# A tile and a queue of their own for the raw rows of the seven-product units in an FFN down projection

## The chip, the cores and the metric

The kernel runs on one core of one Trainium2 chip. The metric is the device time of one execution in microseconds (us), as the median of several runs. The engines are named as the profile names them: PE is TensorE's matmul side and PEld its weight loads, DVE is VectorE, ACT is ScalarE, POOL is GpSimd, SP is SyncE, which issues most of the DMA loads.

## What is computed

One layer of a decoder trunk over 256 tokens of width 2048, all in float32: a norm, a combined projection, two attentions, gated merging and an output product, then a convolutional gated FFN. The change lies in the FFN's last product. Cut to what matters:

```
def conv_ffn(h, w_up, conv_w, conv_b, w_down):
    a, b = jnp.split(h @ w_up, 2, axis=-1)
    c = conv_b + sum(conv_w[j] * shifted(a, j) for j in range(3))
    return (gelu(c) * b) @ w_down          # (256, 5632) @ (5632, 2048)

x = x + rms_norm(conv_ffn(rms_norm(x, norm_ffn_pre), ...), norm_ffn_post)
```

## The kernel before, in words

**Precision.** Every float32 operand is split into a high part in the fp32r format and a low part, the rest. ScalarE makes the high part (`convert`, L143, "whi"), VectorE subtracts it from the raw values (L144, "wlo"). A product of two split operands is three matmuls: high by high (L175), high by low (L176) and low by high (L177), in `mm3`.

**Order.** The kernel is written with a tile framework. The text of the program gives an order, and the framework's scheduler then orders the instructions of each engine from priorities and modelled times; every engine runs its own list strictly in that order and waits on semaphores. Tiles come from pools: a tile with a tag and `bufs` slots may be written only when the earlier tile in its slot has had all its reads. A helper `at(t, f)` puts off small pieces of work to a later `tick()`; each plain weight row of the stage and each half of a unit of seven ends with one tick.

**Weights.** A raw weight tile holds 128 rows by 1024 columns (512 KB). `raw_row` (L147 to L152) takes one from a ring of three slots (`RAW`) and lets SP load it (L151). Its high and low parts come from rings of four slots (`RING`) with two more under a shared tag; which of raw and converted tiles has these two is set by `flex`, and in the FFN it is the converted ones.

**The FFN.** The up product runs in eleven column blocks of 512 (`ffn_up`), the down product in two parts. After block 5, 24 of the 44 row blocks of w_down are used by `down_pair`, for two pairs of 512 columns each (p = 0 and p = 1); after block 10 the other 20 row blocks follow, and the final norm, whose scale is `gpost2`.

**`down_pair`.** The 24 row blocks are taken in twelve units of two rows. For one unit the product is a 2 x 2 product of blocks: two token halves by two row blocks, and two row blocks by two column halves.
- A *plain* unit (from L1110) converts its two rows and makes 8 products, 24 matmuls, into four accumulators c.
- A unit of *seven* products makes 21 matmuls, by a scheme of the Strassen kind. From its raw rows `even` and `odd` VectorE forms the four differences ta and tb (L1124 to L1127; L1127 writes tb's second half from `odd` and tb's first half). Converted are `odd` whole, the first half of `even`, ta and tb. The products are, in this order: c11 and c12 with odd; q1 with even; q5 and q7 with ta; q6 and c21 with tb. The token sums s1 to s4 that stand on the other side were made earlier (`token_sums`), for the row units 0 to 3; they lie in tiles that take the place of the residual x2.
- After the last unit of seven of a pair, the four q accumulators are combined into the output tiles (L1141 to L1145, "ds"). At the end of the pair the four c accumulators are added (L1155).
- In pair 0 the c accumulators are in the four PSUM banks of the pool `pacc` and the q accumulators in the four others; in pair 1 they are exchanged. The up product's first accumulators ("ua") take `pacc`, its second ("ub") the four others, and are evicted by L1062 and L1063.

The order of the units was the same for both pairs, `PAIR_ORDER = "psppsppsppsp"`, p for plain and s for seven: four units of seven in each pair.

**Around it.** The residual x2 is stored to memory during block 2 by GpSimd (`park`, L1007) and loaded again by SP after the pairs (`unpark`, L1013), as soon as the token sums have been used. GpSimd also loads the scale `gpost2` (L1077) right after block 0, into the tile with the tag "gp", which the scale of the attention's output norm had before. ta and tb share their slots (tags "fa" and "fb") with the evicted up accumulators.

Of the kernel before, what the change touches and what calls it, by code (L numbers as in the profile page):

```python
# [19 lines left out]
P = 128  # L20
D = 2048
# [20 lines left out]
def trunk_layer(ctx, tc, x, x_cols_in, conv_cols_in, g_mix_post, g_ffn_post, w_in, w_q, w_kv,  # L42
                sinks, rel, wo_a, wo_b, w_out, w_up, w_down, rope_tab, strip_sel, out):
    nc = tc.nc
    vec, act, pe, pool = nc.vector, nc.scalar, nc.tensor, nc.gpsimd

    def open_pool(name, bufs=1, **kw):
        es = ExitStack()
        return es, es.enter_context(tc.tile_pool(name=name, bufs=bufs, **kw))
# [9 lines left out]
    def sb(pl, shape, name, dt=F32, tag=None, bufs=None):  # L59
        return pl.tile(shape, dt, name=name, tag=tag or name, **({"bufs": bufs} if bufs else {}))  # L60
# [46 lines left out]
    def ring_tile(kind, name, dt, extra):  # L107
        pl_tag = dict(name=name, tag="flex", bufs=2) if extra else dict(name=name, tag=kind, bufs=RAW if kind == "raw" else RING)
        return ring.tile([P, 1024], dt, **pl_tag)

    def in_turn(kind):

        turn[kind] += 1
        return flex[0] == kind and turn[kind] % (RAW + 2 if kind == "raw" else RING + 1) >= (RAW if kind == "raw" else RING)
# [32 lines left out]
    def raw_row(src):  # L147
        i = cnt[0]
        cnt[0] += 1
        raw = ring_tile("raw", f"raw{i}", F32, in_turn("raw"))  # L150
        nc.sync.dma_start(raw, src)  # L151
        return raw  # L152
# [7 lines left out]
    def tick():  # L160
        for f in steps.pop(now[0], ()):
            f()
        now[0] += 1
# [15 lines left out]
    def gemm(xh, xl, w, k0, nk, c0, n, split=None, extra=None, ps=None):  # L179

        kc = 1024 // n if n in (256, 512) else 2
        acc = new_acc("g", ps)
        todo = []
        cuts = list(range(0, nk, kc)) + [nk]
        for ci, (k, ke) in enumerate(zip(cuts[:-1], cuts[1:])):
            kk = ke - k
            src = w[(k0 + k) * P:(k0 + k + kk) * P, c0:c0 + n].rearrange("(a p) n -> p a n", p=P)
            hi, lo = wchunk(src, [kk, n], *(extra or {}).get(ci, ()))
            for j in range(kk):
                kt = k + j  # L190
                wh, wl = hi[:, j * n:(j + 1) * n], lo[:, j * n:(j + 1) * n]
                for t in range(NT):
                    x_ = [x(k0 + kt)[:, t * P:(t + 1) * P] for x in (xh, xl)]
                    if split is None or t == 0 or ci < split:
                        mm3(acc[t][:, :n], *x_, wh, wl, kt == 0, kt == (split * kc if split and t else nk) - 1)
                    else:
                        todo.append((kt, x_, wh, wl))
            tick()
        return acc, todo
# [377 lines left out]
    acc, _ = gemm(XH, XL, w_in, 0, KT, 0, 512)  # L577
# [4 lines left out]
    acc, _ = gemm(XH, XL, w_in, 0, KT, C_KV, KVR + ROPE)  # L582
# [201 lines left out]
    for j in range(4):  # L784
        acc, _ = gemm(XH, XL, w_in, 0, KT, C_GA + 512 * j, 512)
# [15 lines left out]
    es6, p6 = open_pool("p6")  # L801
# [33 lines left out]
    for j in range(4):  # L835
        ld = merge_loads(j)
        acc, _ = gemm(AH, AL, wo_a, 0, KT, 512 * j, 512)
# [124 lines left out]
    def ffn_up0():  # L962

        sa = [[None, None], [None, None]]

        def evac(acc, q):
            f = sb(p6, [P, 1024], f"f{q}_0", tag="f" + "ab"[q], bufs=2)
            for t in range(NT):
                a = f[:, t * 512:(t + 1) * 512]
                act.activation(a, acc[t], AF.Copy, scale=rf[t][q][:, 0:1])  # L970
                sa[t][q] = a

        def cols(i):
            pt = pst.tile([P, 512], F32, name=f"fT{i}", tag="t")
            for q in range(2):
                for t in range(NT):
                    pe.transpose(pt[:, q * 256 + t * P:q * 256 + (t + 1) * P], sa[t][q][:, i * P:(i + 1) * P], ident)
            conv_cols(i, pt[:, 0:256], pt[:, 256:512], i)

        acc, todo = gemm(HH, HL, w_up, 0, KT, 0, 512, split=0, extra=first_extra)  # L980
        finish_tile(acc[1], todo)
        x2_norm(0)
        x2_norm(1)
        evac(acc, 0)
        drain()
        es8.close()
        esx.close()
        es7, p7 = open_pool("p7")
        g = [slot("b", i) if i < 8 else sb(p7, [P, 1024], f"ghl{i}", F32R) for i in range(12)]
        gT[0][:], gT[1][:] = highs(g), lows(g)  # L990
        dsum_all[:] = [sb(p7, [P, D], f"ds{t}") for t in range(NT)]
        dsum[:] = [[d[:, j * 512:(j + 1) * 512] for j in range(4)] for d in dsum_all]
        norm_row()
        for p in range(8):
            at(now[0] + 1 + (3 * p) // 2, lambda p=p: normed(p, p7))
        acc, _ = gemm(HH, HL, w_up, 0, KT, DFF, 512, ps=(pss, "s"))
        evac(acc, 1)
        for i, w in enumerate((1, 2, 4, 6)):
            at(now[0] + w, lambda i=i: cols(i))
        gtiles[:] = g  # L1000
        s_pool.append(p7)
        return es7
# [70 lines left out]
            at(now[0] + 1 + 2 * i, lambda i=i: conv_cols(4 * c + i, sa[0][i], sa[1][i], slot0 + i))  # L1073

    es7 = ffn_up0()
    gpost2 = sb(p6, [P, D], "gpost2", tag="gp")
    pool.dma_start(gpost2, g_ffn_post.partition_broadcast(P))  # L1077
    for c in range(1, 6):
        if c == 2:
            for i in range(8):  # L1080
# [15 lines left out]
    def down_pair(p):  # L1096

        c11, c12, c21, c22 = c = banks(p, f"c{p}_")
        q1, q5, q7, q6 = q = banks(1 - p, f"q{p}_")
        j0, used = 2 * p, set()  # L1100
        d = [dsum[t][j0 + j] for t in range(NT) for j in range(2)]
        act_of = lambda k, t: (GH(k)[:, t * P:(t + 1) * P], GL(k)[:, t * P:(t + 1) * P])
        row = lambda k: w_down[k * P:(k + 1) * P, j0 * 512:(j0 + 2) * 512]
        half = lambda w, i: tuple(x[:, i * 512:(i + 1) * 512] for x in w)

        def mul(o, x, w, last=False):
            mm3(o, *x, *w, id(o) not in used, last)
            used.add(id(o))

        def plain(u, last):  # L1110
            for k in (2 * u, 2 * u + 1):
                w = convert(raw_row(row(k)), 1024)
                for t in range(NT):
                    for j in range(2):
                        mul(c[2 * t + j], act_of(k, t), half(w, j), last and k % 2 == 1)
                tick()

        def seven(u, last):
            s1, s2, s3, s4 = s_of[u]
            even, odd = raw_row(row(2 * u)), raw_row(row(2 * u + 1))  # L1120
            ta, tb = (sb(p6, [P, 1024], f"t{n}{p}_{u}", tag="f" + n, bufs=2) for n in "ab")
            lo_, hi_ = slice(0, 512), slice(512, 1024)
            w = convert(odd, 1024)
            vec.tensor_tensor(ta[:, lo_], even[:, hi_], even[:, lo_], op=ALU.subtract)  # L1124
            vec.tensor_tensor(ta[:, hi_], odd[:, hi_], even[:, hi_], op=ALU.subtract)
            vec.tensor_tensor(tb[:, lo_], odd[:, hi_], ta[:, lo_], op=ALU.subtract)
            vec.tensor_tensor(tb[:, hi_], odd[:, lo_], tb[:, lo_], op=ALU.subtract)  # L1127
            mul(c11, act_of(2 * u + 1, 0), half(w, 0))
            mul(c12, s4, half(w, 1))
            w = convert(even, 512)  # L1130
            mul(q1, act_of(2 * u, 0), half(w, 0), last)
            w = convert(ta, 1024)
            mul(q5, s1, half(w, 0), last)
            mul(q7, s3, half(w, 1), last)
            tick()
            w = convert(tb, 1024)
            mul(q6, s2, half(w, 0), last)
            mul(c21, act_of(2 * u + 1, 1), half(w, 1))
            tick()
            if last:  # L1140
                act.copy(d[0], q1)  # L1141
                vec.tensor_tensor(d[1], d[0], q6, op=ALU.add)
                vec.tensor_tensor(d[2], d[1], q7, op=ALU.add)
                vec.tensor_tensor(d[3], d[2], q5, op=ALU.add)
                vec.tensor_tensor(d[1], d[1], q5, op=ALU.add)  # L1145

        plain_of, seven_of = iter(range(4, 12)), iter(range(4))
        for i, kind in enumerate(PAIR_ORDER):
            if kind == "s":
                u = next(seven_of)  # L1150
                seven(u, u == 3)
            else:
                plain(next(plain_of), i == len(PAIR_ORDER) - 1)
        for o, x in zip(d, c):
            vec.tensor_tensor(o, o, x, op=ALU.add)  # L1155

    for p in range(2):
        down_pair(p)
    for i in range(8):
        at(now[0] + 40 + 2 * i, lambda i=i: unpark(i // 4, i % 4))  # L1160
    for c in range(6, 11):
# [65 lines left out]


RING = 4
PAIR_ORDER = "psppsppsppsp"  # L1230
XCUT = [0, 1, 2, 3, 4, 6, 8, 10, 12, 14, 16]
X_LOAD = [0, 1, 2, 3, 4, 6, 7, 8, 10]
X_SQ = [4, 4, 5, 5, 6, 7, 8, 9, 10, 11]
# [71 lines left out]
```

## Time and profile before

| What | us |
|---|---|
| median of 3 runs | 1475.07 (1475.04 to 1475.78) |
| the profiled execution's own time | 1475.35 |
| its span in the profile | 1473.5 |
| stage of the two pairs, first product of c to first product of the next ua | 1003.91 to 1132.44 |
| start of the second pair | 1066.49 |

The span is what the profile shows of the program; the 1.85 us between it and the execution's own time lie before and after it. Times within the span are counted from its start. The clock that TensorE was granted is 1.00 in the stage.

How its lines are read: a group or timeline row has the line, the engine, the operation, the tile written, an arrow, the tiles read, the shape, and xN for the number of instructions merged. In the timeline the first number is the start and the second the duration; square brackets hold how long the engine had been idle and what ended that. A matmul's duration is a modelled one of some 0.39 us with the next one overlapping it, so the pace of TensorE is read from the distance of two starts. A row of the waits says who waited for whom, how long in total, how many times, and the longest. SPq is SP's queue of DMA issues; in a row of DMA issues the last number is the median time from issue to landing.

### The profile page before, as it was taken

What the parts mean: (1) busy time and instruction counts of PE and PEld (TensorE: products, weight loads), DVE (VectorE), ACT (ScalarE), POOL (GpSimd) and SP (SyncE); (2) the same over time, 40 slices, a digit from 0 to 9 for tenths busy, and PEclk for the clock granted to TensorE, in tenths of its full rate; (3) what the DMA queues carried; (4) which work ended last, traced back from release to release, by engine and by line L of the source; (5) the groups of instructions that cost most, each with busy time, mean ns of one, the idle gap of its engine ahead of it and who ended that gap; (6) DMA issues with size and microseconds to landing.
All of it is one profiled execution on the core that took longest, in us unless ns stands there. A gap on an engine that the chain in (4) does not pass through costs nothing.

```text
span 1473.5 us, 20861 instructions
## 1 busy us (share of the span) xinstructions
PE 1460.6 (99%) x7591; PEld 1246.1 (85%) x7591; DVE 1026.6 (70%) x1799; ACT 818.3 (56%) x1354; POOL 51.1 (3%) x87
## 2 busy tenths in 40 slices
PE   9999999999999999999999999999999999999997
PEld 7888888888888888888888888888877888888886
DVE  7788874445667665555799877677777676677556
ACT  7588864444565554444666565555444565565443
POOL 0021100000000010000000000000000000000000
PEclk9999999999999999999999999999999999999999
DMA  8755376666655559755766666665667666666653
GB/s 291 223 171 165 94 219 195 206 209 200 186 160 156 171 163 339 224 197 195 224 202 184 192 193 185 188 196 162 209 199 226 210 200 190 194 186 187 198 189 126
DMA packets 154513, 287.58 MB, mean 195 GB/s; under 512 B 18427, under 2 KB 29596, under 8 KB 154284
## 3 DMA queue, kind: packets, MB, share of 16 engines
q1 hardware_dynamic: 149664, 270.43, 59.4%
q0 software_dynamic: 4656, 15.78, 3.4%
q8 instruction: 59, 0.97, 0.3%
q14 instruction: 42, 0.34, 0.1%
q10 hardware_dynamic: 92, 0.05, 0.0%
HBM read 277.79 MB, written 8.44 MB: 194 GB/s over the span
## 4 chain that ended last, share of the span: by engine, by line
PE 92%; DVE 3%; DMA 3%; ACT 1%; issue 0%; DVEq 0%; ACTq 0%; SPq 0%
PE accg L175 15%; PE accg L177 15%; PE accg L176 15%; PE ub L1041 10%; PE ua L1041 10%; PE ua L1045 5%; PE ub L1045 5%; DMA raw<-in_ffn_w_down_dram 2%; PE c L175 1%; PE c L176 1%; PE c L177 1%; DVE wlo L144 1%; PE mpo L760 1%; PE ms L726 1%; PE pt L442 1%; PE qn L691 1%
## 5 line engine op out<-in xcount | busy, mean ns | idle before, releaser
L144 DVE TENSOR_TENSOR wlo<-raw,whi 128x1024 fp32r<-128x1024 f32 (+2 forms) x502 | 604.7, 1207 | 345.4 <-ACT whi L143 340.6
L143 ACT CAST whi<-raw 128x1024 fp32r<-128x1024 f32 (+2 forms) x502 | 518.6, 1036 | 495.7 <-PE accg L177 239.2
L175 PE MATMUL accg<-whi,ahl 128*128 128x512 f32 (+1 forms) x544 | 212.9, 391 | 0.0
L177 PE MATMUL accg<-whi,ahl 128*128 128x512 f32 (+1 forms) x544 | 210.5, 387 | 0.0
L176 PE MATMUL accg<-wlo,ahl 128*128 128x512 f32 (+1 forms) x544 | 209.7, 385 | 0.0
L175 PE MATMUL accg<-whi,bhl 128*128 128x512 f32 x442 | 173.0, 391 | 0.0
L177 PE MATMUL accg<-whi,bhl 128*128 128x512 f32 x442 | 172.3, 390 | 0.0
L176 PE MATMUL accg<-wlo,bhl 128*128 128x512 f32 x442 | 172.2, 390 | 0.0
L1041 PE MATMUL ua<-ahl,whi 128*128 128x512 f32 x640 | 154.8, 391 | 0.9 <-DVE ds L1145 0.9
L1041 PE MATMUL ub<-ahl,whi 128*128 128x512 f32 x640 | 154.6, 391 | 0.0
L1041 PEld LDWEIGHTS ua<-ahl,whi 128*128 128x128 f32 x640 | 117.4, 188 | 24.0 <-DVE ds L1145 1.3
L1041 PEld LDWEIGHTS ub<-ahl,whi 128*128 128x128 f32 x640 | 117.5, 188 | 22.9 <-ACT cc L930 0.3
L177 PEld LDWEIGHTS accg<-whi,ahl 128*128 128x128 f32 x544 | 102.1, 188 | 20.6
L176 PEld LDWEIGHTS accg<-wlo,ahl 128*128 128x128 f32 x544 | 102.3, 188 | 18.1
L175 PEld LDWEIGHTS accg<-whi,ahl 128*128 128x128 f32 x544 | 102.3, 188 | 17.9
L177 PEld LDWEIGHTS accg<-whi,bhl 128*128 128x128 f32 x442 | 83.0, 188 | 17.4
L175 PEld LDWEIGHTS accg<-whi,bhl 128*128 128x128 f32 x442 | 83.0, 188 | 16.9
L176 PEld LDWEIGHTS accg<-wlo,bhl 128*128 128x128 f32 x442 | 83.0, 188 | 16.8
L1045 PEld LDWEIGHTS ub<-ahl,wlo 128*128 128x128 f32 x640 | 82.2, 191 | 3.2
L1045 PEld LDWEIGHTS ua<-ahl,wlo 128*128 128x128 f32 x640 | 82.2, 191 | 3.1
L1045 PE MATMUL ua<-ahl,wlo 128*128 128x256 f32 x640 | 83.7, 283 | 0.0
L1045 PE MATMUL ub<-ahl,wlo 128*128 128x256 f32 x640 | 83.2, 283 | 0.0
(409 smaller groups left out, 1876.1 us busy)
## 6 DMA issues: line engine op xcount, KB each, us to landing
raw<-in_ffn_w_up_dram SPq DMA_DIRECT2D x176, 512.0 KB, 4.5
raw<-in_w_in_dram SPq DMA_DIRECT2D x111, 512.0 KB, 4.4
raw<-in_ffn_w_down_dram SPq DMA_DIRECT2D x88, 512.0 KB, 4.3
raw<-in_w_o_swa_dram SPq DMA_DIRECT2D x32, 512.0 KB, 4.3
raw<-in_w_o_mla_dram SPq DMA_DIRECT2D x32, 512.0 KB, 4.8
raw<-in_w_out_dram SPq DMA_DIRECT2D x32, 512.0 KB, 4.2
bias<-strip POOLq DMA_DIRECT2D x16, 256.0 KB, 4.3
raw<-in_mla_w_q_up_dram SPq DMA_DIRECT2D x32, 128.0 KB, 2.6
```

The lines of the kernel that those rows point to most:

```text
L143: act.copy(hi[:, a:b], raw[:, a:b])
L144: vec.tensor_tensor(lo[:, a:b], raw[:, a:b], hi[:, a:b].bitcast(F32), op=ALU.subtract)
L175: pe.matmul(o, ah, bh, start=start, stop=False)
L176: pe.matmul(o, ah, bl, start=False, stop=False)
L177: pe.matmul(o, al, bh, start=False, stop=stop)
L442: pe.transpose(pt[:, j * P:(j + 1) * P], p[:, c * P:(c + 1) * P], ident)
L691: pe.matmul(o, wl, ch(k), start=False, stop=k == nk - 1)
L726: pe.matmul(o, w, v_, start=n == 0, stop=False)
L760: pe.matmul(o, w(t), p_[:, c], start=n == 0, stop=n == 5)
L1041: pe.matmul(acc[i], hi[:, c], hn[p][:, j * 512:(j + 1) * 512], start=p + j == 0, stop=stop)
L1045: pe.matmul(acc[i][:, 0:256], lo[:, c], hn[p][:, j * 512:j * 512 + 256], start=False, stop=False)
```

## The change

The two raw rows of a unit of seven lie side by side in one tile of 128 x 2048 under the tag "gp" (one slot), and GpSimd loads them as two DMAs of 512 KB. So that the tag is free, the scale's load moves behind both pairs. The order of the units becomes one string for each pair: the first begins with a unit of seven and has four, the second begins with a plain unit as before, has three, and ends on four plain units. The row blocks that are no longer used by a unit of seven go to plain units. All else is the same.

```diff
     es7 = ffn_up0()
-    gpost2 = sb(p6, [P, D], "gpost2", tag="gp")
-    pool.dma_start(gpost2, g_ffn_post.partition_broadcast(P))
     for c in range(1, 6):
...
         def seven(u, last):
             s1, s2, s3, s4 = s_of[u]
-            even, odd = raw_row(row(2 * u)), raw_row(row(2 * u + 1))
+            both = sb(p6, [P, D], f"rr{p}_{u}", tag="gp")
+            even, odd = both[:, 0:1024], both[:, 1024:2048]
+            pool.dma_start(even, row(2 * u))
+            pool.dma_start(odd, row(2 * u + 1))
...
-        plain_of, seven_of = iter(range(4, 12)), iter(range(4))
-        for i, kind in enumerate(PAIR_ORDER):
+        sevens = PAIR_ORDER[p].count("s")
+        plain_of, seven_of = iter(range(sevens, 12)), iter(range(sevens))
+        for i, kind in enumerate(PAIR_ORDER[p]):
             if kind == "s":
                 u = next(seven_of)
-                seven(u, u == 3)
+                seven(u, u == sevens - 1)
             else:
-                plain(next(plain_of), i == len(PAIR_ORDER) - 1)
+                plain(next(plain_of), i == len(PAIR_ORDER[p]) - 1)
...
     for p in range(2):
         down_pair(p)
+    gpost2 = sb(p6, [P, D], "gpost2", tag="gp")
+    pool.dma_start(gpost2, g_ffn_post.partition_broadcast(P))
...
-PAIR_ORDER = "psppsppsppsp"
+PAIR_ORDER = ("sppsppsppspp", "psppsppspppp")
```

In the orders that the scheduler makes, the loads of the first unit's rows stand on GpSimd among the stores of the residual, near where the scale's load stood; the loads of the other six units follow one after another, then the scale's. On SP 14 loads of raw rows are gone and the reloads of the residual stand some places earlier, among the last row loads of pair 1. At the front of pair 0 VectorE has the first unit's odd and even rows and ta ahead of the four evictions of ub, and L1127 and tb's low part behind them; TensorE has one high-part matmul of c21 ahead of q6's low-part one, and three of the next plain row ahead of its first low-part one.

## The prediction

> **What bounds the kernel now.** I read the page first: its span, its busy shares, and the shares of the chain that ended last.
>
> ```profile
> span 1473.5 us, 20861 instructions
> PE 1460.6 (99%) x7591; PEld 1246.1 (85%) x7591; DVE 1026.6 (70%) x1799; ACT 818.3 (56%) x1354; POOL 51.1 (3%) x87
> PE 92%; DVE 3%; DMA 3%; ACT 1%; issue 0%; DVEq 0%; ACTq 0%; SPq 0%
> ```
>
> TensorE carries the end. The change can pay only where TensorE waits inside the stage it touches, the two column pairs of the FFN down product, and it costs at least whatever matmuls it adds. So next I split that stage at the first product of the second pair (windows: time, PE busy, PEld, DVE, ACT, POOL, clock, DMA share, GB/s).
>
> ```profile
> 1003.91:1066.49 62.58, 62.58 (x278) 51.82 (x277) 50.06 (x63) 32.43 (x40) 0.00 (x0) 1.00 0.60 190
> 1066.49:1132.44 65.95, 64.14 (x277) 51.47 (x276) 48.13 (x54) 31.18 (x33) 0.00 (x0) 1.00 0.64 200
> ```
>
> By the code each pair has 8 plain units of 24 matmuls and 4 units of seven products with 21: 276. (The counts include one or two of the neighbours.) The first pair takes 62.58 us, 0.2267 us per matmul. The second, same work and clock 1.00, takes 65.95: **3.37 us of waiting, all in the second pair**. Who is waited for is in TensorE's waits from 1003 to 1136 us, and two of them in the timeline:
>
> ```profile
> PE c L176 <- DVE wlo L144: 1.6, 2, 0.8
> PE ua L1041 <- DVE ds L1145: 0.9, 1, 0.9
> PE q L176 <- DVE wlo L144: 0.2, 1, 0.2
> 1120.71 0.50 PE L175 MATMUL c<-whi,bhl 128*128 128x512 f32 x1
> 1122.02 0.50 PE L176 MATMUL c<-wlo,bhl 128*128 128x512 f32 x1 [0.80 <-DVE wlo L144]
> 1122.35 0.39 PE L177 MATMUL c<-whi,bhl 128*128 128x512 f32 x1
> 1132.44 0.84 PE L1041 MATMUL ua<-ahl,whi 128*128 128x512 f32 x3
> 1134.20 1.42 PE L1041 MATMUL ua<-ahl,whi 128*128 128x512 f32 x5 [0.92 <-DVE ds L1145]
> 1135.46 0.76 PE L1045 MATMUL ua<-ahl,wlo 128*128 128x256 f32 x5
> ```
>
> Starts count, not the modelled idle time: 1120.71 to 1122.02 is 1.31 instead of 0.23, and the matmul after a wait takes 0.33. A fourth wait lies just behind the stage: eight matmuls from 1132.44 to 1135.46 take 3.02 instead of 8 x 0.2267 = 1.81, so **1.21 us**. Together 4.58 us.
>
> Why is the low part (wlo) late? The chain of waits before 1122 says it, with what SP's queue waited for in the second pair:
>
> ```profile
> 1113.51 6.00 DMA raw<-in_ffn_w_down_dram
> 1119.53 0.69 DVE ta L1125
> 1120.22 0.60 DVE tb L1126
> 1120.82 1.14 DVE wlo L144
> 1121.96 0.61 DVE tb L1127
> 1122.63 4.02 DMA raw<-in_ffn_w_down_dram
> SPq L151 <- DVE wlo L144: 30.0, 14, 5.5
> SPq L151 <- DVE tb L1127: 8.0, 4, 3.0
> SPq L1013 <- PE c L177: 1.1, 2, 0.9
> ```
>
> The raw ring has three tiles in this stage. A unit of seven takes two of them and holds both until L1127 and the low parts have read them; four waits of SP end at L1127. So the unit's second row is asked for only at 1113.51, lands 6 us later, and VectorE, which stands in order, stops at L1125.
>
> **The change, part by part.** Line numbers are those of the kernel before.
>
> *One unit fewer.* The order goes from eight units of seven to seven: 21 matmuls become 24, 3 x 0.2267 = **+0.68 us** on the path, certain.
>
> *Own tile.* 14 of the stage's 48 row loads leave SP's ring of three; it then serves plain rows alone, one per 12 x 0.2267 = 2.72 us of TensorE. What a ring slot costs comes from these rows (issues: count, KB, median us to landing; groups: busy, mean ns, idle):
>
> ```profile
> raw<-in_ffn_w_down_dram SPq DMA_DIRECT2D x88, 512.0 KB, 4.3
> L143 ACT CAST whi<-tb 128x1024 fp32r<-128x1024 f32 x8 | 8.4, 1054 | 5.2 <-DVE tb L1127 3.8 <-PE c L177 1.4
> L144 DVE TENSOR_TENSOR wlo<-tb,whi 128x1024 fp32r<-128x1024 f32 x8 | 9.8, 1221 | 0.4 <-ACT whi L143 0.3
> L1127 DVE TENSOR_TENSOR tb<-raw,tb 128x512 f32<-128x512 f32 x8 | 5.5, 684 | 0.0
> ```
>
> Load, high part, low part: 4.3 + 1.05 + 1.22 = 6.6 us, over three slots 2.2 us per row, under 2.72. With the 6.00 us load it is 8.3, or 2.8: short only by 0.04 per row. VectorE is no rival bound: 98.2 of 128.5 us busy, and it loses a unit's work (five 512-wide subtractions at 0.68 and three of 1024 at 1.22, 7.1 us, against 2.4 for two plain rows). So the three row-bound waits go: **-3.37**. The other end is that none of it goes (0). I take the full value, because TensorE's order shows no other producer there.
>
> *Last unit earlier.* Pair 1 now ends on eight plain rows after its last unit instead of two, 21.8 us, so the four combinations that free the banks (L1142 to L1145, 0.68 each) are over long before the up product needs them: **-1.21**. What is late next there is the addition of the c banks, which the following up accumulators don't use.
>
> *First unit at the very front of pair 0.* Here cover is lost. TensorE comes to the unit with nothing between, and VectorE's new order puts L1127 behind the four evictions of the up banks. Rows:
>
> ```profile
> 1003.91 0.39 PE L175 MATMUL c<-whi,bhl 128*128 128x512 f32 x1
> 1003.43 1.21 ACT L1062 ACTIVATE f<-ub 128x256 f32<-128x256 f32 x4 [2.41 <-PE ub L1041]
> 1003.84 1.42 DVE L1063 SCALAR_TENSOR_TENSOR f<-ub,f 128x256 f32<-128x256 f32 x4 [1.17 <-ACT f L1062]
> 1005.18 0.42 DVE L938 TENSOR_TENSOR uu<-uu,f 128x256 f32<-128x256 f32 x1
> ```
>
> The evictions end at 1005.2; L1127 to 1005.9; ScalarE's high part of tb (1.05) to 1007.0; the low part (1.22) to 1008.3. TensorE has 15 matmuls that don't need tb, and the new order puts two high-part matmuls ahead of the first low one: 1003.91 + 17 x 0.2267 = 1007.76. It waits 0.5, plus 0.1 for the slow matmul after a wait: **+0.65**. Bounds: 0 if everything runs a little earlier, 1.4 if VectorE begins only when ScalarE has evicted all four banks (1004.64). The next plain row's low part stands one short subtraction behind tb's, at 1009.8, and TensorE's order covers that one too.
>
> *GpSimd's queue.* The first unit's rows are asked for during the stores near 740 us and are there 260 us early. The other six reloads wait on GpSimd until the unit before has read the tile; nothing else stands behind them there but the scale's load, first read in the last stage. Nearest rows:
>
> ```profile
> lyb<-yb_d POOLq DMA_DIRECT2D x8, 256.0 KB, 5.0
> x_d<-x POOLq DMA_DIRECT2D x8, 256.0 KB, 5.9
> gpost<-in_norm_ffn_post_dram POOLq DMA_DIRECT2D x1, 1024.0 KB, 4.8
> DMA to landing us min/median/max: 4.5/5.9/6.5
> 738.03 0.54 POOL L1077 DMA_DIRECT2D gpost<-in_norm_ffn_post_dram  x1 [8.74 <-DVE ry_u L222]
> 1083.03 0.62 ACT L143 CAST whi<-raw 128x512 fp32r<-128x512 f32 x1 [1.66 <-DMA raw<-in_ffn_w_down_dram]
> ```
>
> (The fourth row is that of the stores to x_d, the slowest of GpSimd's.) I take 5 us for the first half row pair and 6 for the second (issued 0.54 later); bounds 4 (just under the shortest of that row) and 10 (two of 5 in line). What the new wait holds up: VectorE stands in order, and behind L1124 and L1125 stand low parts of plain rows. Tightest is the second unit: tile free at 1005.9, and ahead of the fourth plain row stand the high parts of the unit (1.05 + 0.62), that row's own (1.05) and its low part (1.22), while TensorE comes to it at about 1017.7. So the second half may land as late as 1013.7, 7.8 us after the request; 1.8 us to spare. Later units: a turn is load plus some 6.7 us of reading against 69 x 0.2267 = 15.6 us between units, which allows 9 us. So 0.
>
> The Trainium skill speaks against this queue: SBUF — State Buffer, section "SBUF: two separate sides", says that GpSimd cannot write its descriptors while VectorE is in a two-port mode, and the section after it tells of a load of some 0.62 us that took 3.1. By that figure, an estimate, 2.5 us more would bring the second half to 8.5 us and cost 0.7 once. The stage's VectorE rows are two-input subtractions, which the page's "Who interferes with whom" counts among those that did not stall a load; no run here shows the blocked case.
>
> *SP's order.* The eight loads of the stored residual (256 KB each) move ahead of the next up rows, the last of them now falling within pair 1's tail. They wait for the last use of the token sums; before, SP lost 1.1 us to that. Three ring slots and the low parts already made cover it: 0, at worst 1.
>
> Sum: 0.68 + 0.65 - 3.37 - 1.21 = **-3.25 us**, on the profiled execution's own 1475.35 us (span 1473.5), 0.28 above the median of 1475.07. From the median: 1471.8.
>
> **The rivals.**
> - *Some of the waits stay, or small ones take their place* in the second pair: residual loads (2 MB), scale (1 MB) and units' rows now crowd into its last 40 us, and rows that land in 6 us leave the ring just short. Half of 4.58 kept: -1.0, so 1474.1. For it: 200 GB/s there already. Against: after a unit the ring has 4.8 us of TensorE time in which no plain row is used.
> - *The change doesn't do what it says*: the rows were late for another reason, only the matmuls and the front wait are added: +0.7 + 0.65, so 1476.4. Against: the L1127 releases above.
> - *The other side:* GpSimd's loads become the period. The place is VectorE's stop at L1124 and L1125. Of the six reloads the first costs what it lands beyond 7.8 us, each of the other five what it lands beyond 9. At 10 us that is 2.2 + 5 x 1.0 = 7.2, so 1471.8 + 7.2 = 1479; slower than before from about 9.4 us on. For it: every one of these loads is asked for at the moment when SP's own are under way, at 190 to 200 GB/s. Against: no store or load of GpSimd's above took over 6.5 us.
>
> **How the numbers follow.** Forecast 0.60 (1471.2 with no front wait to 1472.9), waits partly stay 0.24 (1472.9 to 1475.0), not doing what it says 0.08, GpSimd's period 0.08. The range, 1471.2 to 1475.1, holds the first two. About what a measurement of this kernel can tell from no change is 0.2%, 2.95 us, so faster begins under 1472.12: three quarters of the forecast, 0.45. Slower (over 1478.0) gets 0.07, nearly all of the last case. The rest is 0.48.
>
> **What would show it.** Right: 279 matmuls' time more or less nothing over 0.2267 each in pair 1 (279 x 0.2267 = 63.3 us), no wait of ua at the stage's end, one wait of about 0.5 us at q's low part some 3.9 us into pair 0, GpSimd's loads landing in 4 to 7 us, L1124 and L1125 free of waits that reach TensorE. Wrong: waits of c for wlo in pair 1, loads over 8 us, or SP stopped at the residual loads.

## The result, and the profile after

The changed kernel takes **1479.60 us** (median of 8 runs, 1478.99 to 1483.99) where the kernel before takes 1475.03 beside it (8 runs, 1474.57 to 1475.78): ratio 1.0035, 95% interval 1.0024 to 1.0046. It is slower; the forecast was 1471.8. The profiled execution took 1478.99 us, 3.64 more than the one before.

The lines of `seven` have moved by one: the differences of ta and tb are L1125 to L1128 in the changed kernel. First the page: span, busy shares, and the shares of the chain that ended last.

```profile
span 1477.0 us, 20859 instructions
PE 1461.7 (99%) x7594; PEld 1247.0 (84%) x7594; DVE 1022.1 (69%) x1793; ACT 816.2 (55%) x1352; POOL 58.5 (4%) x101
PE 92%; DVE 3%; DMA 2%; ACT 1%; issue 1%; POOL 0%; DVEq 0%; ACTq 0%
```

Nothing stands out here: three matmuls more, and the same engine bound. The stage has to be split, at the first product of the second pair (windows, columns as before the change: time, busy PE, PEld, DVE, ACT, POOL, clock, DMA share, GB/s).

```profile
1003.79:1070.18 66.39, 64.03 (x278) 51.45 (x276) 53.38 (x68) 34.61 (x43) 4.21 (x8) 1.00 0.59 194
1070.18:1137.34 67.16, 64.18 (x281) 52.16 (x279) 44.33 (x48) 29.73 (x31) 2.63 (x5) 1.00 0.69 227
```

The first pair has 276 matmuls, 62.6 us at 0.2267, and takes 66.39: it had no wait before, now it has 3.8 us. The second has 279, 63.25 us, and takes 67.16: 3.9 us of waits, where the forecast was none. The clock is 1.00 in both. Who waits for whom, in the waits of TensorE and of VectorE in the stage:

```profile
PE c L176 <- DVE wlo L144: 3.3, 4, 1.4
PE q L176 <- DVE wlo L144: 1.9, 2, 1.5
DVE ta L1125 <- DMA rr<-in_ffn_w_down_dram: 12.7, 5, 4.7
DVE ta L1126 <- DMA rr<-in_ffn_w_down_dram: 1.5, 2, 0.9
```

TensorE waits for low parts of both kinds, VectorE for the new tile's loads, 14.2 us. The wait of ua for the ds at the stage's end is gone. The loads themselves are no longer than the forecast took them to be (issues: count, KB, median us to landing); read one by one they landed 3.7 to 6.6 us after their issue.

```profile
raw<-in_ffn_w_down_dram SPq DMA_DIRECT2D x74, 512.0 KB, 4.4
rr<-in_ffn_w_down_dram POOLq DMA_DIRECT2D x14, 512.0 KB, 4.9
```

How a load of ordinary length comes to cost something is seen in one place of the changed kernel's timeline: GpSimd, then VectorE, ScalarE and TensorE.

```profile
1049.72 0.53 POOL L1120 DMA_DIRECT2D rr<-in_ffn_w_down_dram  x1 [15.35 <-DVE wlo L144]
1049.34 1.22 DVE L144 TENSOR_TENSOR wlo<-ta,whi 128x1024 fp32r<-128x1024 f32 x1
1054.45 0.69 DVE L1125 TENSOR_TENSOR ta<-rr 128x512 f32<-128x512 f32 x1 [3.89 <-DMA rr<-in_ffn_w_down_dram]
1055.06 1.22 DVE L144 TENSOR_TENSOR wlo<-tb,whi 128x1024 fp32r<-128x1024 f32 x1
1058.12 2.35 DVE L144 TENSOR_TENSOR wlo<-raw,whi 128x1024 fp32r<-128x1024 f32 x2
1049.65 1.06 ACT L143 CAST whi<-tb 128x1024 fp32r<-128x1024 f32 x1 [0.81 <-PE c L176]
1052.60 1.05 ACT L143 CAST whi<-raw 128x1024 fp32r<-128x1024 f32 x1 [1.89 <-PE c L177]
1057.59 0.39 PE L175 MATMUL c<-whi,ghl 128*128 128x512 f32 x1
1059.39 0.50 PE L176 MATMUL c<-wlo,ghl 128*128 128x512 f32 x1 [1.42 <-DVE wlo L144]
```

The unit has just been read, so at 1049.72 GpSimd asks for the next one. VectorE's list has the next unit's first difference (L1125) right there, even ahead of the *current* unit's low part of tb. VectorE stands from 1050.56 to 1054.45. The high part of tb is done at 1050.71 and that of a plain row at 1053.65; their low parts could follow at once, and run at 1055.06 and 1058.12. TensorE comes to that plain row's low part some 0.23 after 1057.59 and gets it at 1059.39.

### The profile page after: what moved, and what is told of

Its sections match the earlier page's. It is cut to its first block, busy times and chain, and to the rows that moved or that the text cites. A ratio compares the mean times of both kernels' runs of the same rounds, so it can differ in the third digit from the quotient of the medians.

```text
span 1477.0 us, 20859 instructions
## 1 busy us (share of the span) xinstructions
PE 1461.7 (99%) x7594; PEld 1247.0 (84%) x7594; DVE 1022.1 (69%) x1793; ACT 816.2 (55%) x1352; POOL 58.5 (4%) x101
## 4 chain that ended last, share of the span: by engine, by line
PE 92%; DVE 3%; DMA 2%; ACT 1%; issue 1%; POOL 0%; DVEq 0%; ACTq 0%
PE accg L175 15%; PE accg L177 15%; PE accg L176 15%; PE ua L1041 10%; PE ub L1041 10%; PE ub L1045 5%; PE ua L1045 5%; DVE wlo L144 2%; PE c L176 1%; PE c L177 1%; PE c L175 1%; DMA rr<-in_ffn_w_down_dram 1%; DMA raw<-in_ffn_w_down_dram 1%; PE mpo L760 1%; PE ms L726 1%
## 5 line engine op out<-in xcount | busy, mean ns | idle before, releaser
L144 DVE TENSOR_TENSOR wlo<-raw,whi 128x1024 fp32r<-128x1024 f32 (+2 forms) x488 | 592.0, 1216 | 347.3 <-ACT whi L143 342.2
L143 ACT CAST whi<-raw 128x1024 fp32r<-128x1024 f32 (+2 forms) x488 | 507.1, 1042 | 486.3 <-PE accg L177 247.2
```

The lines of the kernel that those rows point to most:

```text
L143: act.copy(hi[:, a:b], raw[:, a:b])
L144: vec.tensor_tensor(lo[:, a:b], raw[:, a:b], hi[:, a:b].bitcast(F32), op=ALU.subtract)
```

## The experiments

The theory: VectorE's *order* turns the load into a wait. A single tile is asked for only when the unit before has been read; a difference of the next unit that stands directly behind in VectorE's list makes VectorE stand until the load has landed, and ready low parts stand behind it. Rivals: GpSimd's queue is slow or blocked; the order of the units costs by itself; one tile gives too long a turn whatever VectorE's order. The kernel before ran beside every group; its medians there were 1474.66, 1474.07, 1474.68 and 1474.14 us. Ratios are against it, with the 95% interval.

**The order of the units alone**, rows still in SP's ring:

```diff
-PAIR_ORDER = "psppsppsppsp"
+PAIR_ORDER = ("sppsppsppspp", "psppsppspppp")
```

> Only the order and number of the units is changed; raw rows stay in SP's ring of three. Theory A (VectorE's list has the next unit's first differences ahead of plain rows' low parts, stands there for GpSimd's load, and the ring of plain rows is held up behind it): nothing of that is here, so 0.7 for the three matmuls, some 0.6 at the front, -1.2 at the stage's end, and the second pair's waits about as before: 1474 to 1476. Rival C (the new order itself costs the time): 1478 to 1480.

Measured: 1477.04 us, ratio 1.0015 (1.0006 to 1.0024). That is about 1 us over what was expected. By the distances of its starts TensorE waits 5.4 us for low parts behind the front, against 3.37 before, and VectorE stands at the differences here too, for rows of the ring.

```profile
DVE ta L1125 <- DMA raw<-in_ffn_w_down_dram: 7.3, 5, 2.3
DVE ta L1124 <- DMA raw<-in_ffn_w_down_dram: 1.9, 3, 0.8
```

The wait of ua is gone, as the forecast had it. The order gains that and loses more. It explains about half of the loss (2.4 of 4.6 us by the medians).

**The tile and its queue alone**, with the old order:

```diff
-PAIR_ORDER = ("sppsppsppspp", "psppsppspppp")
+PAIR_ORDER = ("psppsppsppsp", "psppsppsppsp")
```

> Own tile and GpSimd's queue as in the changed kernel, but the order before, eight units. Theory A and rival B (GpSimd's loads, or the one slot, are too slow whatever VectorE's order): seven reloads instead of six, the stage's end wait is back, the front wait and 0.7 of matmuls are gone: 1478 to 1481. Rival C: under 1474.

Measured: 1481.24 us, 1.0045 (1.0032 to 1.0057), with three matmuls fewer than the changed kernel. With the old order the tile alone loses more than the whole change does. Its waits of VectorE are longer than the changed kernel's:

```profile
DVE ta L1125 <- DMA rr<-in_ffn_w_down_dram: 18.5, 7, 4.7
```

**The changed kernel with SP's queue** for the tile's loads:

```diff
-            pool.dma_start(even, row(2 * u))
-            pool.dma_start(odd, row(2 * u + 1))
+            nc.sync.dma_start(even, row(2 * u))
+            nc.sync.dma_start(odd, row(2 * u + 1))
```

> The changed kernel with the units' rows loaded by SP instead of GpSimd. Theory A: landing takes about as long on SP (4.4 against 4.9 us), VectorE still stops, and SP itself now stands in order before the plain rows' loads until the tile is free: 1479 to 1486. Rival B in the form that GpSimd's queue is the slow part: 1472 to 1475.

Measured: 1479.07 us, 1.0028 (1.0017 to 1.0040). The queue is not the cause: from SP's queue the loads land no sooner, and VectorE stands as long.

```profile
rr<-in_ffn_w_down_dram SPq DMA_DIRECT2D x14, 512.0 KB, 5.0
DVE ta L1125 <- DMA rr<-in_ffn_w_down_dram: 13.3, 4, 4.9
```

**The changed kernel with VectorE's order held.** The scheduler gets one edge: the two differences of ta may be placed only behind the last low part that the text makes ahead of the unit. Both instructions are on VectorE, so the edge changes an order only. The traces bear that out: by the tiles named in their rows, TensorE's and SP's lists are in the stage those of the changed kernel, and ScalarE's differs in the place of one small activation.

```diff
-            vec.tensor_tensor(lo[:, a:b], raw[:, a:b], hi[:, a:b].bitcast(F32), op=ALU.subtract)
+            low_part[0] = vec.tensor_tensor(lo[:, a:b], raw[:, a:b], hi[:, a:b].bitcast(F32), op=ALU.subtract)
...
             pool.dma_start(odd, row(2 * u + 1))
...
+            with tc.issue_after(low_part[0].ins):
+                vec.tensor_tensor(ta[:, lo_], even[:, hi_], even[:, lo_], op=ALU.subtract)
+                vec.tensor_tensor(ta[:, hi_], odd[:, hi_], even[:, hi_], op=ALU.subtract)
             w = convert(odd, 1024)
-            vec.tensor_tensor(ta[:, lo_], even[:, hi_], even[:, lo_], op=ALU.subtract)
-            vec.tensor_tensor(ta[:, hi_], odd[:, hi_], even[:, hi_], op=ALU.subtract)
```

> The changed kernel, with a unit's two first differences held behind the low part of the plain row that stands ahead of the unit in the program (an ordering edge on VectorE alone; same tile, queue, order and number of units). Theory A: VectorE no longer stops for GpSimd's load, the waits of c and q for low parts inside the pairs go, 0.6 at the front stays: 1471.5 to 1473. Rival B: the load is as late as before, 1478 to 1480. Rival C: no change, 1478 to 1480.

Measured: 1473.23 us, 0.9991 (0.9982 to 1.0000); 6.4 us below the changed kernel with the same tile, queue, units and loads. VectorE has no wait for a DMA left in the stage, and all that TensorE waits for is the front wait that the prediction had put at 0.65 us (starts 0.67 us too far apart):

```profile
PE q L178 <- DVE wlo L144: 0.4, 1, 0.4
```

**The edge alone, on the kernel before**, and **the held version with other orders of the units** (eight units of seven; or seven with a plain unit in front):

```diff
-PAIR_ORDER = ("sppsppsppspp", "psppsppspppp")
+PAIR_ORDER = ("psppsppsppsp", "psppsppsppsp")
```

```diff
-PAIR_ORDER = ("sppsppsppspp", "psppsppspppp")
+PAIR_ORDER = ("psppsppsppsp", "psppsppspppp")
```

> The kernel before (raw rows in SP's ring, eight units) with one edge alone: the two ta differences may be issued only after the low part that precedes the unit in the text. If VectorE's order, with a difference that waits for a load ahead of plain low parts, made the 3.37 us of waits in the second pair already, they go: 1471.3 to 1472.5, the ua wait of 1.21 at the stage's end stays. If the ring of three slots is the bound, as the prediction had it, they stay: 1474 to 1476.

Measured: 1474.71 us, 1.0003 (0.9994 to 1.0012), runs from 1472.99 to 1476.67: no gain. VectorE still stops for rows of the ring:

```profile
DVE ta L1127 <- DMA raw<-in_ffn_w_down_dram: 7.9, 5, 1.9
DVE ta L1126 <- DMA raw<-in_ffn_w_down_dram: 3.2, 4, 1.2
```

In its one profiled execution (1473.33 us, near its quickest) few of the waits for low parts are left (1.3 us in the stage) and ua's is; why the median doesn't show that is open.

> The changed kernel with its own tile and GpSimd's queue, VectorE's order held, and the old order of eight units in both pairs. If the held order is all that the tile needs, with the turn between two units down to 69 matmuls in both pairs: no load waits, 3 matmuls less (0.68) and no front wait (0.6) than the held version's 1473.2: 1471.3 to 1472.5, with up to 1.2 back if ua waits at the stage's end. If the tile itself is too slow a turn for eight units: 1474 to 1478, with waits of DVE for rr.

Measured: **1471.30 us**, 0.9981 (0.9972 to 0.9990). With the rows above this is a table of two by two for eight units of seven: neither 1, tile alone 1.0045, edge alone 1.0003, both 0.9981. By the medians neither gains anything without the other. In the held version with eight units no matmul of the stage waits; each pair takes 276 x 0.2267 us:

```profile
1004.31:1066.87 62.56, 62.56 (x278) 51.82 (x276) 50.38 (x64) 33.78 (x42) 4.21 (x8) 1.00 0.58 194
1066.87:1129.45 62.58, 62.58 (x278) 51.73 (x276) 49.65 (x57) 30.92 (x32) 3.68 (x7) 1.00 0.66 220
```

The same place in its list as above: a plain row's low part, then the differences without a stop (the load of 1038.15 has been there for 6 us), and only then GpSimd's next request.

```profile
1048.17 1.23 DVE L144 TENSOR_TENSOR wlo<-raw,whi 128x1024 fp32r<-128x1024 f32 x1 [2.09 <-ACT whi L143]
1049.31 0.68 DVE L1127 TENSOR_TENSOR ta<-rr 128x512 f32<-128x512 f32 x1
1054.09 0.53 POOL L1122 DMA_DIRECT2D rr<-in_ffn_w_down_dram  x1 [14.89 <-DVE tb L1131]
```

> The held version, seven units, with the first pair in the old order, so that a plain unit stands ahead of the first unit of seven. The front wait of q for tb's low part (0.6 us) goes, nothing else: 1472.0 to 1473.2, and a stage with 0.0 to 0.5 us of waits in all. If the unit's place at the front is not what makes that wait, as the held version: 1473.2 with the wait in another place.

Measured: 1472.15 us, 0.9987 (0.9978 to 0.9996), no wait in the stage. The front wait comes from the unit's place at the front; three matmuls more than eight units, 0.68 us, account for most of the 0.85 between the two.

**No reloads**, VectorE's order left to the scheduler:

```diff
-            both = sb(p6, [P, D], f"rr{p}_{u}", tag="gp")
-            even, odd = both[:, 0:1024], both[:, 1024:2048]
-            pool.dma_start(even, row(2 * u))
-            pool.dma_start(odd, row(2 * u + 1))
+            if not kept:
+                kept.append(sb(p6, [P, D], "rr", tag="gp"))
+                for i in range(2):
+                    pool.dma_start(kept[0][:, i * 1024:(i + 1) * 1024], row(2 * u + i))
+            even, odd = kept[0][:, 0:1024], kept[0][:, 1024:2048]
```

> The changed kernel, but the raw rows of the first unit of seven are loaded once and every unit of seven reads them: 12 loads of 512 KB are left out, and the sums of the later units are made from the wrong rows. VectorE's list is left to the scheduler, which again puts differences ahead of plain low parts. If VectorE's stop for the reloads costs the time: no wait of ta, 1472 to 1474. If the differences' mere place, or SP's ring, costs it: 1477 to 1480.

Measured: 1472.59 us, 0.9992 (0.9983 to 1.0001), one wait of 0.6 us at the front. Differences ahead of plain low parts cost nothing when they need not wait. So it takes both, the early place and the load. (Twelve loads fewer also leave the DMA engines freer; the held version, which has all the loads and the same gain, speaks against that as the cause.)

**A longer load.** The tile loaded twice in line, in the changed kernel and in the held version with eight units:

```diff
-            pool.dma_start(even, row(2 * u))
-            pool.dma_start(odd, row(2 * u + 1))
+            for i in (1, 0):
+                pool.dma_start(even, row(2 * u + i))
+                pool.dma_start(odd, row(2 * u + 1 - i))
```

> The changed kernel, but each unit's tile is loaded twice in line (first with its two rows exchanged, then as it should be), so that the last half should land some 9 to 10 us after the request instead of 5. If VectorE's stop at the next unit's differences carries the loss, each of some five stops grows by 4 to 5 us, and TensorE, which in the changed kernel loses 6.9 us to 14.2 us of stops, loses about half of that too, or all of it where no row is left: 1489 to 1503. If the loss comes from something else in the new order, such as SP's bursts: 1479 to 1483.

> The held version with eight units, each tile loaded twice in line, so that the last half should land 9 to 10 us after the request. In the held version with eight units VectorE comes to the next unit's differences 9.7 to 18.5 us after the request (1107.88 was the latest landing, 5.7 us after it). If the held order gives the load that much room, the doubled load costs little: 1471.3 to 1474. If the turn of one tile was already short, with every microsecond of loading on the path: 7 units by 4.5 us, 1485 to 1503.

Measured: 1504.20 us, 1.0203 (1.0187 to 1.0218), just over its range, and 1496.52 us, 1.0148 (1.0131 to 1.0165), in the range of the load that lies wholly on the path. The dose was larger than expected: the second loads took mostly 7 to 9 us, so the first reload's last half landed 14.4 and 15.8 us after the first request. With some 5 us of reading that is a turn of about 20 us, as the first requests of the held version show (1008, 1028, 1050, 1069, 1089, 1106, 1126), against 15.6 us of TensorE time; four to five too long, six times, is the 25 us lost. At this size the turn bounds both orders, and the pair doesn't tell the theories apart.

**A small delay instead**, strips of 128 x 128 ahead of the two loads, in the same two kernels:

```diff
-            pool.dma_start(even, row(2 * u))
-            pool.dma_start(odd, row(2 * u + 1))
+            for n in (128, 1024):
+                pool.dma_start(even[:, :n], row(2 * u)[:, :n])
+                pool.dma_start(odd[:, :n], row(2 * u + 1)[:, :n])
```

> The changed kernel, with two strips of 128 x 128 loaded into the unit's tile ahead of its two loads, which must wait for them: the rows should land some 2 to 3 us later, 7 to 8 us after the request. If VectorE's stop at the next unit's differences carries the loss, six stops grow by 2 to 3 us and about half of that reaches TensorE, as in the changed kernel (6.9 of 14.2): 6 to 9 us, 1485 to 1489. If only the turn of the tile counts (load plus 4.7 us of reading against 15.6 us between units), nothing: 1479 to 1481.

> The same two strips ahead of the loads in the held version with eight units. The turn by the doubled load's trace is the load plus some 4.7 us, so rows that land up to 10.9 us after the request still fit into the 15.6 us between units: 1471.3 to 1473 (nothing, or one small wait). If each microsecond of loading reaches TensorE whatever the order: seven reloads by 2 to 3 us by a half or more, 1478 to 1490.

Measured: 1485.22 us, 1.0074 (1.0060 to 1.0088), and 1479.39 us, 1.0041 (1.0028 to 1.0053). The first lies in its range, but in part by luck. VectorE's stops for the tile grew from 14.2 to 19.8 us, less than half of the growth expected (six by 2 to 3 us), and TensorE's waits by some 2 us. Some 3 us more come from TensorE's clock, which fell to half twice (last section); the expectation did not have that.

```profile
DVE ta L1126 <- DMA rr<-in_ffn_w_down_dram: 14.5, 5, 5.0
DVE ta L1127 <- DMA rr<-in_ffn_w_down_dram: 5.3, 4, 3.0
```

The second is a miss: the held version loses 8.1 us where nothing or one small wait was expected. Its loads landed late, most of the second halves 10 to 11 us after the first request. And most of the stop for the tile is now on another engine, ScalarE:

```profile
ACT whi L143 <- DMA rr<-in_ffn_w_down_dram: 21.3, 7, 8.1
1037.46 1.05 ACT L143 CAST whi<-rr 128x1024 fp32r<-128x1024 f32 x1 [7.38 <-DMA rr<-in_ffn_w_down_dram]
1038.41 1.04 ACT L143 CAST whi<-raw 128x1024 fp32r<-128x1024 f32 x1
```

The next unit's high part stands ahead of a plain row's in ScalarE's list. The edge on VectorE moves the point at which a load begins to cost; it doesn't remove it. Counted from the first request to the landing of the second half, that point was at most 5.8 us in the changed kernel (the load of 1033.32, with a wait of TensorE right behind its stop). In the held version with eight units it lies somewhere between 6.1 us (its latest landing, no wait) and 10 to 11. Whether ScalarE's place sets it was not tried. The turn of the tile may set it as well: the first requests of this run lie 14.9 to 18.5 us apart, against 15.6 us of TensorE time between units, and no run parts the two.

**The held version with eight units, SP's queue:**

```diff
-            pool.dma_start(even, row(2 * u))
-            pool.dma_start(odd, row(2 * u + 1))
+            nc.sync.dma_start(even, row(2 * u))
+            nc.sync.dma_start(odd, row(2 * u + 1))
```

> The held version with eight units, the unit's rows loaded by SP's queue instead of GpSimd's. In SP's list a load that waits for the tile stands ahead of the plain rows' loads behind it. If GpSimd's own queue is worth something once VectorE's order is held, waits of c for plain rows come back: 1473 to 1478. If the queue doesn't matter, as it did not in the changed kernel: 1471.3 to 1472.5.

Measured: 1471.10 us, 0.9977 (0.9968 to 0.9986), no wait in the stage: the same as with GpSimd's queue. Both versions beat both kernels.

## Why the prediction was wrong

- *One unit fewer, +0.68*: right. 555 matmuls instead of 552.
- *Last unit earlier, -1.21*: right. Nine starts of ua behind the stage take 1.81 us, and no wait of ua is left.
- *First unit at the front, +0.65*: right in place and size. At 1007.41 the next start is 0.73 us away instead of 0.23 and the one behind it 0.34: 0.61 us.
- *Own tile, -3.37*: **wrong, in sign**. The waits for low parts other than the front one went from 3.37 to 6.9 us, +3.55. Of the 6.9 us, 6.6 stand right behind VectorE's stops for the tile; the rest, at 1017.79, stands behind a plain row that landed late. With the three terms above, 0.68 - 1.21 + 0.61 + 3.55 = 3.63 us; the profiled executions differ by 3.64.

The step that failed is "Later units: a turn is load plus some 6.7 us of reading against 69 x 0.2267 = 15.6 us between units, which allows 9 us. So 0." The sum asks whether the tile comes round in time for TensorE. It doesn't ask where in VectorE's list the next difference stands, and the place was named a few sentences ahead: "VectorE stands in order, and behind L1124 and L1125 stand low parts of plain rows." Only the second unit's list was followed to its end, and there the difference stood behind enough other work. For later units the scheduler puts the difference close behind the unit before, where the load has just been asked for. Then a load of ordinary length is a stop too: VectorE stood 3.89 and 4.69 us of the 4.7 and 5.5 us that the first half took in the two worst places. The third rival had the place and, as a turn, the wrong threshold (9.4 us): halves that landed 4.0 to 6.6 us after their issue made the kernel slower.

A second gap lies in the kernel before. Its waits of VectorE in the same stage had the sign already:

```profile
DVE ta L1125 <- DMA raw<-in_ffn_w_down_dram: 9.4, 6, 2.8
DVE ta L1124 <- DMA raw<-in_ffn_w_down_dram: 2.3, 4, 0.8
```

The prediction saw one of these stops (1119.53) and put it down to the raw ring alone, so that a tile of its own would end it. It took both: by the medians the tile without the edge, and the edge without the tile, bring no gain.

With the order held, the seven-unit version's profiled span is 1470.5 us, 3.0 below the span before, where the sum said 3.25: between these two executions the sum comes out once the order is held. Its median gains 1.4 us only, not 3. The kernel before varies between 1472.6 and 1476.3 us, and its profiled execution, 1475.35, lies in the upper part; the held version's, 1472.58, lies 0.65 us below its own median. So the 4.58 us of waits is one execution's and probably more than the typical one has, and the prediction's gain was also read too large.

*GpSimd's queue.* The loads landed about as estimated (first halves 3.9 to 5.5 us after their issue, second halves 4.6 to 6.6), and the rule of the Trainium skill (SBUF — State Buffer, "SBUF: two separate sides") that was weighed against this queue did not show: in both orders SP's queue gives nearly the same time as GpSimd's. This agrees with the Trainium skill's DMA: Bandwidth & Descriptors, "Issuing engines are not separate DMA queues", that DMAs run on the same engines whoever starts them.

## What to carry to other kernels

When a buffer is reloaded, ask two things: does its turn fit between two uses, and what stands directly behind its first reader in that engine's own list. An in-order engine that comes to the reader early stands until the load has landed, and what is late is the ready work behind it. A scheduler may need to be told that order. The held version with the strips suggests that this goes for every engine that reads the buffer; that was not tried.

## What the hardware showed unasked

**TensorE's clock fell after short waits.** In the changed kernel with the strips, a matmul waited from 1085.75 to 1088.22 (2.5 us from start to start). The next 1.5 us ran at full clock, and then 3 us at half (windows as above; the seventh figure is the granted clock, and starts there are 0.427 us apart):

```profile
1085.70:1088.20 2.50, 0.44 (x2) 0.01 (x1) 2.00 (x4) 1.04 (x1) 0.00 (x0) 1.00 0.03 10
1088.20:1089.70 1.50, 1.48 (x6) 1.24 (x7) 1.50 (x2) 0.00 (x0) 0.00 (x0) 1.00 0.26 41
1089.70:1092.70 3.00, 3.00 (x9) 2.29 (x8) 3.00 (x4) 0.83 (x1) 0.00 (x0) 0.51 0.88 270
```

So a wait of 2.5 us cost 2.2 and then some 1.6 us more. The wait of 4.1 us in the same execution (starts at 1043.38 and 1047.50) was followed, from 1048.79 on, by 3.4 us at a clock of 0.50. In the changed kernel itself, whose longest wait is 1.9 us from start to start, the clock stayed at 1.00 in the stage. The Trainium skill (TensorE: Matmul & The Clock Gate, "Part 1: The HAM clock gate") puts the half clock after an idle window of about 3.4 us; the half clock and the some 3 us to come back agree, but here the shorter of the two waits, 2.5 us, was shorter than that window.

**A small load is not a cheap one.** The strips of 64 KB took 2.2 us to land, half of what 512 KB took in the same stage:

```profile
rr<-in_ffn_w_down_dram POOLq DMA_DIRECT2D x12, 64.0 KB, 2.2
rr<-in_ffn_w_down_dram POOLq DMA_DIRECT2D x12, 512.0 KB, 4.4
```
